# A decoder layer on one core: strided queries of the dilated attention copied, keys and values stored in runs of four tokens

## The chip, the cores and the metric

The kernel runs on one core of a Trainium2 chip. The metric is the device time of one launch in microseconds, the median of the runs shown. All arithmetic is in 32-bit floats (fp32, and fp32r for most products).

## The reference, cut to what matters

One inference step of one layer, for a prompt of 2048 tokens (width 1024) and for eight samples of four tokens. A normed input is projected to q, k, v and u; q, k, v feed an attention of 8 heads of 64, u a pooling mixer; then an output projection, a second norm and a convolutional feed-forward. The change touches the prompt's attention. It has three patterns per head, with dilation 1, 4 and 16: a query sees itself and up to 128 earlier tokens of the same residue. The core of it, cut:

```python
DIL_PATTERNS = ((128, 1), (512, 4), (2048, 16))

def _dilated_branch_prompt(q, k, v, dilation, slopes):
    qs = q.reshape(b, L, dilation, h, dh)          # L = s // dilation
    ...
    kb = jnp.concatenate([kp[:, :-1], kp[:, 1:]], axis=2)   # the block before, the block itself
    scores = jnp.einsum('bnqchd,bnkchd->bnchqk', qb, kb).astype(jnp.float32) * (HEAD_DIM ** -0.5)
    diff = qi + Q_BLOCK - ki
    valid = ((diff >= 0) & (diff <= N_STRIDED))[None] & (key_j >= 0)
    bias = -slopes[:, None, None] * (dilation * diff).astype(jnp.float32)[None]
    scores = jnp.where(valid[None, :, None, None], scores + bias[None, None, None], NEG)
    m = jnp.max(scores, axis=-1, keepdims=True)
    p = jnp.exp(scores - m)
    l = jnp.sum(p, axis=-1, keepdims=True)
    out = jnp.einsum('bnchqk,bnkchd->bnqchd', (p / l).astype(v.dtype), vb)
```

The three patterns are then merged with weights from their log-sums.

## The kernel before, in words

**Projection.** Sixteen tiles of 128 tokens are normed, turned and multiplied with W_in (`project`, three products per pair of 128 rows, high and low parts). `finish_qk` (L444) norms q and k per head; `spill_qk` (L466) turns a tile so that channels stand on the partitions, splits it into high and low part (ScalarE L472, VectorE L474) and stores both in DRAM (`qT_hi`, `qT_lo`, `kT_hi`, `kT_lo`, 512 x 2048). `finish_v` (L434) stores v row by row (`v_s`).

**Attention.** For a head, `load_head` (L227) brings queries and keys of all 2048 tokens into one tile `QK` (two such tiles): high and low parts of the queries one above the other, and the keys' high and low part, each twice. A pattern has sixteen blocks of 128 queries: pattern 0 sixteen consecutive blocks, pattern 1 four blocks of each of four residues, pattern 2 one block of each of sixteen residues. `views` (L238) cuts a block's operands out of the tile by a stride: one float in 4 (16 bytes) for pattern 1, one in 16 (64 bytes) for pattern 2. A block that has a predecessor reads 256 keys, one without 128; pattern 2 has no predecessors at all, pattern 1 in 12 of 16 blocks, pattern 0 in 15.

An item is two blocks of one head and pattern; 8 items make a pattern, 192 the stage. `advance(i)` (L310) issues three steps of three items:

- `scores` (L248) of item i: per block two products, queries as the stationary operand (loaded as weights), keys high and then low as the moving one (L262, L263); VectorE adds the bias table, whose columns are keys, and reduces a row to its minimum (L265); ScalarE takes the exponential (L267). Buffers: Sp 4, T 4, P 4.
- `turn` of item i-2: a transpose of each 128 x 128 of P (L275), copied out of PSUM by VectorE or, every fourth time, ScalarE (L278, L280).
- `values` of item i-3: the products with V (L296, two passes each); ScalarE copies the output (L300), GpSimd the row minima (L302, `st` to O); every fourth item of an odd head stores O (`store_o`).

Items go by head, pattern 0, 1, 2 (2, 1, 0 in the last head). The loop at L656 also issues the loads: the next head's queries and keys, V of the next pair of heads (`next_v`, `load_v` L176: pattern 0 one DMA, pattern 1 four, pattern 2 one, in rows of 512 bytes), rows of the feed-forward's parameters (tile `row`, three buffers) and parts of W_out (`rawo`, same buffers). SP issues nearly all DMAs, in order. GpSimd makes the bias table (L166), the ones beside V (L172, L173) and the copies of L302.

The rest (merge, output projection, feed-forward by chunks of 512 tokens, the sample group's attention in between) is not touched.

Of the kernel before, what the change touches and what calls it, by code (L numbers as in the profile page):

```python
# [9 lines left out]
F32 = mybir.dt.float32  # L10
# [7 lines left out]
P = 128  # L18
# [25 lines left out]
def kernel(ctx, tc, ins, cst, outs):  # L44
# [25 lines left out]
    # the sample group's columns of a product stand side by side, hi then lo: one pass takes both  # L70
# [23 lines left out]
    def norm_rows(pool, xt, g_bc, bufs, tag="xn"):  # L94
        """x * rsqrt(mean(x^2) + eps), times g_bc where given."""
        rows = xt.shape[0]
        xn = pool.tile([rows, DM], F32, tag=tag, name="xn", bufs=bufs)
        ss = pool.tile([rows, 1], F32, tag="ss", name="ss", bufs=2)
        nc.scalar.activation(xn, xt, AF.Square, accum_out=ss)
        r = rms_scale(pool, ss, 1, DM)  # L100
        if g_bc is None:
            nc.scalar.activation(xn, xt, AF.Copy, scale=r)
        else:
            nc.vector.scalar_tensor_tensor(out=xn, in0=xt, scalar=r, in1=g_bc[:rows], op0=ALU.mult, op1=ALU.mult)  # L104
        return xn
# [5 lines left out]
    def transpose_split(src, hi, lo):  # L111
        """src [n, DM] -> hi, lo [128, KT, n]."""
        n = src.shape[0]
        for h in range(2):
            tp = psum.tile([P, 4, P], F32, tag="tp", name="tp", bufs=4)
            for k in range(4):
                kk = 4 * h + k
                nc.tensor.transpose(tp[:, k, :n], src[:, kk * P:(kk + 1) * P], ident[:n, :n])  # L118
            split(hi[:, 4 * h:4 * h + 4, :], lo[:, 4 * h:4 * h + 4, :], tp[:, :, :n])
# [8 lines left out]
    class Later:  # L128
        """Work on the tensor engine that is issued some bursts of products after what it waits for."""
# [39 lines left out]
    def value_tile(pool, tag):  # L169
        """Pairs of heads, with a column of ones on either side (the sums of the weights)."""  # L170
        t = pool.tile([P, 16, P + 2], F32, tag=tag, name="V", bufs=3 if tag == "V" else 1)
        nc.gpsimd.memset(t[:, :, 0:1], 1.0)  # L172
        nc.gpsimd.memset(t[:, :, P + 1:P + 2], 1.0)  # L173
        return t

    def load_v(hp, p, t, blocks=slice(0, 16)):  # L176
        vs = v_s[:, hp * P:(hp + 1) * P]
        d = t[:, :, 1:P + 1]
        if p == 0:
            nc.sync.dma_start(d[:, blocks], vs.rearrange("(n i) f -> i n f", i=P)[:, blocks])  # L180
        elif p == 1:
            for J in range(4):
                nc.sync.dma_start(d[:, 4 * J:4 * J + 4, :], vs[J * CH:(J + 1) * CH].rearrange("(i c) f -> i c f", c=4))
        else:
            nc.sync.dma_start(d, vs.rearrange("(i c) f -> i c f", c=16))
# [4 lines left out]
    def param_load(j):  # L190
        n = 2 * NF if j < 4 else 2 * SB
        row = rows_of[j] = p2.tile([2 * NF, 4 * P], F32, tag="row", name="row", bufs=3)
        if j < 4:
            src = conv_b if j == 3 else conv_w[0, j:j + 1]
            nc.sync.dma_start(row[:, 0:P], src.rearrange("l (c p) -> (l c) p", p=P))
        else:
            nc.sync.dma_start(row[:n], stv[:, (j - 4) * 4 * P:(j - 3) * 4 * P])
# [28 lines left out]

    def load_head(h):  # L227
        qk, tab = qk_tile(), bias_table(h)
        load_qk(h, qk, slice(0, S))
        heads[h] = (*(qk[:, i, :] for i in range(3)), tab)  # L230

    pair_v, pair_o, heads = {}, {}, {}
# [4 lines left out]

    def views(h, p, idx):  # L238
        r = DILS[p]
        blk, c = divmod(idx, r)  # L240
        q, kh, kl = (x.rearrange("p (j c) -> p c j", c=r)[:, c, :] for x in heads[h][:3])
        lo = blk - 1 if blk else 0
        return (q[:, blk * P:(blk + 1) * P], kh[:, lo * P:(blk + 1) * P], kl[:, lo * P:(blk + 1) * P],
                ([idx - r] if blk else []) + [idx])
# [3 lines left out]
    def scores(it):  # L248
# [6 lines left out]
        Pt = pq.tile([P, 2, 2 * P], F32, tag="P", name="Pt", bufs=4)  # L255
        blocks = []
        for s in range(2):
# [6 lines left out]
            T = pq.tile([P, 2 * P], F32, tag="T", name="T", bufs=4)  # L264
# [44 lines left out]

    def advance(i):  # L310
        if i < len(items):
            attn[i] = scores(items[i])
        if 0 <= i - 2 < len(items):
            PTs[i - 2] = turn(items[i - 2], attn[i - 2])
        if 0 <= i - 3 < len(items):
            values(items[i - 3], attn.pop(i - 3), PTs.pop(i - 3))

# [1 line left out]
    right = ExitStack()  # L319
    pw = right.enter_context(tc.tile_pool(name="pw", bufs=1, side="right"))  # L320
    with tc.tile_pool(name="p1", bufs=1) as p1:
# [24 lines left out]
        def load_w(i):  # L346
            """Raw weights; the high part of the next ones takes their place."""
# [6 lines left out]
        def split_w(i):  # L354
            """hi + lo of gain * w."""
# [78 lines left out]
        def finish_v(t, j, ps):  # L434
# [3 lines left out]
            else:  # L438
                v = p1.tile([P, AW], F32, tag="t", name="v", bufs=4)
                nc.scalar.copy(v, ps)  # L440
                nc.sync.dma_start(v_s[t * P:(t + 1) * P, :], v)
# [24 lines left out]
        def spill_qk(t, j, a):  # L466
            tp = tp4(a)
            for i, dst in enumerate(((qT_hi, qT_lo), (kT_hi, kT_lo))[j]):
                s = p1.tile([P, 4, P], F32R, tag="qkh", name="qkh", bufs=3)
                if i == 0:  # L470
                    hi = s
                    nc.scalar.copy(hi, tp)  # L472
                else:
                    nc.vector.tensor_tensor(out=s, in0=tp, in1=f32(hi), op=ALU.subtract)  # L474
                nc.sync.dma_start(dst.rearrange("(a p) t -> p a t", p=P)[:, :, t * P:(t + 1) * P], f32(s))

        def window_sums(cur, g, pick, tag, shape, n):
            """Trailing sums over 2 << g columns by doubling; pick(tile, a, b) are the columns a..b-1."""
# [150 lines left out]
    # rows 0..15: the sample group's states (new ones take the place of the old), 16, 17: the prompt's  # L629
# [4 lines left out]
    def h_tile(k):  # L634
        """High and low part of 128 rows: of W_out at first, then of the normed tokens of a chunk."""
# [15 lines left out]
    with tc.tile_pool(name="p2", bufs=1, reuse_waits="tile") as p2:  # L651
# [3 lines left out]
        nc.vector.memset(stT[:, :, 2 * SB:], 0.0)  # L655
        for i in range(AHEAD, len(items) + 3):  # L656
            if i < len(items):
# [23 lines left out]
    with tc.tile_pool(name="p4", bufs=1, reuse_waits="tile") as p4:  # L681
# [163 lines left out]
        def cache_rows(c, b, n, p, near):  # L845
            """The 128 cached rows that query n of sequence b reads in pattern p, as [128, AW]."""
# [139 lines left out]
        def sample_mix():  # L986
            """Output projection, residual and norm of the sample group, then its columns hs_s."""
# [49 lines left out]
        def store_ffn_state(j):  # L1037
            """New states of 512 columns, the sample group's and the prompt's."""
# [18 lines left out]
        for c in range(NCHUNK):  # L1057
# [5 lines left out]
            def spread(pss, prompt, sample):  # L1063
                """Pairs (destination, PSUM source) of the prompt's and sample's columns."""
# [115 lines left out]
def _constants():  # L1180
# [4 lines left out]
    base = np.stack([np.where(ok, r * diff, BIG) for r in DILS]).astype(np.float32)  # L1185
    i = np.arange(P)
# [38 lines left out]
```

## Time and profile before

| | us |
|---|---|
| median of 3 runs | 2590.65 |
| lowest, highest | 2588.75, 2595.58 |
| profiled execution, span from first to last instruction | 2587.3 |
| projection, up to the first score product | 443 |
| attention of the prompt | 399 (443 to 842) |
| merge, output projection, feed-forward | 1745.3 |

Of the profiled execution the profile gives the span; its own time was not taken apart from the runs above. The engines are PE (TensorE products), PEld (its weight loads, which overlap products), DVE (VectorE), ACT (ScalarE), POOL (GpSimd) and SP (the queue that issues DMAs). TensorE is pipelined: the durations of its rows overlap, so the distance from one start to the next says what an instruction costs. A granted clock of 1.00 is 2.4 GHz, 0.50 is 1.2 GHz; a value between is a mean over a stretch.

### The profile page before, as it was taken

To read this page: it belongs to the slowest core of one execution; us is meant where nothing else is said; L and a number is where in the kernel's file an instruction comes from. 1 tells how busy PE (TensorE), PEld (TensorE's weight loads), DVE (VectorE), ACT (ScalarE), POOL (GpSimd) and SP (SyncE) were. 2 spreads that over 40 slices of the span, in tenths; PEclk is the share of its full clock that TensorE was granted. 3 is DMA by queue.
4 is the path that set the end of the run, shared out by engine and by line. 5 is a ranking of instruction groups with operands and counts; after the bars stand their busy time and mean duration, and the time that the engine had idled before them with its cause. 6 is when DMAs were issued, how large, how long until landed. Compare 5 with 4: busy or idle time off the path is not lost.

```text
span 2587.3 us, 35898 instructions
## 1 busy us (share of the span) xinstructions
PE 2556.2 (99%) x13310; PEld 2187.1 (85%) x13310; DVE 1727.8 (67%) x3819; ACT 1089.6 (42%) x2021; POOL 117.4 (5%) x160
## 2 busy tenths in 40 slices
PE   8999999999999999999999999999999999999999
PEld 5888887999999788788888888888888788999997
DVE  7444345555555676799887788887887666666665
ACT  6333232555555222434433464443444443444442
POOL 1111111000000200000000000000000000000000
PEclk9999999998998999999999999999999999999999
DMA  6333335765561897955557534447443337232321
GB/s 220 106 118 112 121 110 149 153 174 131 125 160 51 294 309 244 298 183 183 181 165 233 157 106 146 137 128 246 143 138 114 122 110 232 84 90 83 91 75 61
DMA packets 411738, 393.57 MB, mean 152 GB/s; under 512 B 15211, under 2 KB 318407, under 8 KB 408876
## 3 DMA queue, kind: packets, MB, share of 16 engines
q1 hardware_dynamic: 411340, 390.48, 49.8%
q8 instruction: 105, 1.72, 0.3%
q0 software_dynamic: 224, 0.80, 0.1%
q14 instruction: 69, 0.57, 0.1%
HBM read 305.70 MB, written 85.52 MB: 151 GB/s over the span
## 4 chain that ended last, share of the span: by engine, by line
PE 62%; DMA 1%; DVE 1%; issue 0%; ACT 0%; SPq 0%; POOL 0%; POOLq 0%
PE pu L973 38%; PE pd L1149 19%; PE po L752 3%; PE pd L1143 1%; DMA om<-o_s 0%; DMA h<-hn_s 0%; PE sacc L925 0%; PE sacc L924 0%; PE po L1006 0%; DMA raw<-in_w_up_dram 0%; PE tp L118 0%; DMA h_s<-ya 0%; PE tpf L1041 0%; DVE xn L104 0%; PE tpa L737 0%
## 5 line engine op out<-in xcount | busy, mean ns | idle before, releaser
L973 PE MATMUL pu<-h,w 128*128 128x512 f32 (+1 forms) x5232 | 989.0, 349 | 1.5 <-ACT w L108 1.0
L973 PEld LDWEIGHTS pu<-h,w 128*128 128x128 f32 x5232 | 849.9, 188 | 132.4 <-ACT w L108 1.4
L1149 PE MATMUL pd<-w,act 128*128 128x512 f32 x2112 | 490.2, 392 | 0.0
L1149 PEld LDWEIGHTS pd<-w,act 128*128 128x128 f32 x2112 | 396.6, 188 | 88.1
L108 ACT CAST w<-raw 128x1024 fp32r<-128x1024 f32 (+1 forms) x282 | 286.9, 1026 | 293.0 <-PE pd L1149 189.7
L109 DVE TENSOR_TENSOR w<-raw,w 128x1024 fp32r<-128x1024 f32 (+1 forms) x278 | 328.6, 1185 | 23.9 <-ACT w L108 23.7
L422 PE MATMUL ps<-W_hi,xh 128*128 128x512 f32 x1024 | 332.1, 397 | 1.3 <-ACT xh L108 1.3
L1117 DVE SCALAR_TENSOR_TENSOR cv<-ex,cw,cv 128x512 f32<-128x512 f32 x352 | 262.3, 745 | 29.7 <-ACT cv L1109 27.2
L1107 ACT COPY ex<-pu 128x512 f32<-128x512 f32 (+1 forms) x220 | 110.1, 501 | 350.7 <-PE pu L973 350.3
L265 DVE CUSTOM_DVE_ANT_0 T<-Sp,tab 128x256 f32<-128x256 f32 (+1 forms) x384 | 132.0, 365 | 186.1 <-PE Sp L263 142.2
L422 PEld LDWEIGHTS ps<-W_hi,xh 128*128 128x128 f32 x1024 | 192.2, 189 | 43.4 <-ACT xh L108 2.0
L267 ACT ACTIVATE Pt<-T,st 128x256 f32<-128x256 f32 (+1 forms) x384 | 164.9, 458 | 136.4 <-DVE st L265 134.9
L422 PE MATMUL ps<-W_lo,xh 128*128 128x512 f32 x512 | 202.6, 396 | 0.0
L1151 DVE TENSOR_TENSOR ya<-ya,pd 128x512 f32<-128x512 f32 x192 | 131.0, 683 | 103.7 <-PE pd L1149 102.9
L296 PE MATMUL Op<-V,PTs 128*128 128x65 f32 x1200 | 174.8, 281 | 0.7 <-DVE PTs L278 0.6
L262 PE MATMUL Sp<-QK 128*128 128x256 f32 (+1 forms) x384 | 170.0, 453 | 5.5 <-DMA QK<-kT_hi 3.1
L296 PEld LDWEIGHTS Op<-V,PTs 128*128 128x128 f32 x1200 | 170.0, 209 | 1.2 <-DVE PTs L278 0.7
L1109 ACT ACTIVATE cv<-pu,cw 128x512 f32<-128x512 f32 (+3 forms) x264 | 166.0, 649 | 0.0
L91 POOL TENSOR_TENSOR rs<-ms,mhalf 128x1 f32<-128x1 f32 (+3 forms) x68 | 76.4, 1124 | 1582.7 <-DVE stT L1110 1046.9
L263 PE MATMUL Sp<-QK 128*128 128x256 f32 (+1 forms) x384 | 145.4, 387 | 0.6 <-DMA QK<-kT_lo 0.6
L275 PE MATMUL tp<-ident,Pt 128*128 128x128 f32 x600 | 127.7, 299 | 0.0
L108 ACT CAST act<-cv 128x512 fp32r<-128x512 f32 x88 | 54.6, 621 | 159.4 <-DVE cv L1126 150.7
(220 smaller groups left out, 2637.6 us busy)
## 6 DMA issues: line engine op xcount, KB each, us to landing
raw<-in_w_up_dram SPq DMA_DIRECT2D x176, 512.0 KB
raw<-in_w_down_dram SPq DMA_DIRECT2D x80, 512.0 KB
hn_s<-w SPq DMA_DIRECT2D x16, 1024.0 KB
h<-hn_s SPq DMA_DIRECT2D x32, 512.0 KB
far<-in_cache_k_dram SPq DMA_DIRECT2D x64, 256.0 KB
far<-in_cache_v_dram SPq DMA_DIRECT2D x64, 256.0 KB
om<-o_s SPq DMA_DIRECT2D x16, 792.0 KB
raw<-in_w_in_dram SPq DMA_DIRECT2D x16, 512.0 KB
```

The source lines that it names most:

```text
L108: nc.scalar.copy(hi, src)
L109: (eng or nc.vector).tensor_tensor(out=lo, in0=src, in1=f32(hi), op=ALU.subtract)
L262: nc.tensor.matmul(Sp[:, s, :w], q, kh, start=True, stop=False)
L263: nc.tensor.matmul(Sp[:, s, :w], q, kl, start=False, stop=True)
L265: nc.vector.tensor_tensor_reduce(out=T[:, :w], in0=Sp[:, s, :w], in1=tab[:, p, 2 * P - w:], op0=ALU.add, op1=ALU.min, scale=1.0, scalar=3e ...
L267: nc.scalar.activation(Pt[:, s, :w], T[:, :w], AF.Exp, bias=st[:, i8:i8 + 1], scale=-1.0)
L296: nc.tensor.matmul(Op[:, i4, :], PT[:, j, :], pair_v[hp, p][:, b, v0:v0 + DH + 1], start=n == 0, stop=n == m - 1)
L422: nc.tensor.matmul(ps, xh[:, a, k, :], (W_hi, W_lo)[b][j, k // 2][:, k % 2, :], start=n == 0, stop=n == 3 * KT - 1)
L973: nc.tensor.matmul(ps[:, :n], w[:, a, k, :], hs[k][:, b, c0:c0 + n], start=i == 0, stop=i == 3 * KT - 1)
L1109: nc.scalar.activation(d, s, AF.Identity, bias=cw[:, 3, ct:ct + 1], scale=cw[:, 2, ct:ct + 1])
L1117: nc.vector.scalar_tensor_tensor(out=d, in0=e[j], scalar=cw[:, j, ct:ct + 1], in1=d, op0=ALU.mult, op1=ALU.add)
L1149: nc.tensor.matmul(ps, act[0][:, a, k, tau * P:(tau + 1) * P], wd[k][:, b, :], start=k == 0 and j == 0, stop=k == n - 1 and j == 2)
```

## The change

1. Queries of patterns 1 and 2 are copied by GpSimd, half a pattern (8 blocks, 128 x 1024 floats) at a time, into a tile `qs` (two buffers) in which the tokens of one residue stand in a row. The copy for a half is issued three items before its first item; the two for pattern 1 of head 0 before the loop.
2. Keys are stored in DRAM, and so loaded, in another order: within each 64 tokens, token 16 i + c stands at place 4 c + i. So four tokens of one residue modulo 16 stand in a row, and also four of one residue modulo 4. The order is made where `spill_qk` copies out of PSUM. `views` reads runs of four floats.
3. V is stored in the same order (two DMAs for a tile instead of one). Its loads for patterns 1 and 2 become four DMAs, of 32 partitions each, where there was one.
4. The bias table's columns of patterns 0 and 1 are put in the new order of the keys; pattern 2's order of keys is as before.
5. To make room, T, P and `row` have one buffer less each.

```diff
+RUN = 4
+RES = 16
...
-        elif p == 1:
-            for J in range(4):
-                nc.sync.dma_start(d[:, 4 * J:4 * J + 4, :], vs[J * CH:(J + 1) * CH].rearrange("(i c) f -> i c f", c=4))
         else:
-            nc.sync.dma_start(d, vs.rearrange("(i c) f -> i c f", c=16))
+            r, n = DILS[p], S // (P * DILS[p])
+            for J in range(n):
+                src = vs[J * P * r:(J + 1) * P * r].rearrange("(m c i) f -> i m c f", c=r, i=RUN)
+                for i in range(RUN):
+                    nc.sync.dma_start(d[i::RUN, r * J:r * (J + 1), :], src[i])
...
+    def spread_q(h, p, half):
+        qs = spread[h, p, half] = p2.tile([P, S // 2], F32R, tag="qs", name="qs", bufs=2)
+        q, r = heads[h][0], DILS[p]
+        if p == 1:
+            src = q[:, half * (S // 2):(half + 1) * (S // 2)].rearrange("p (b j c) -> p b c j", b=2, c=r)
+            dst = qs.rearrange("p (b c j) -> p b c j", b=2, c=r)
+        else:
+            src = q.rearrange("p (j c) -> p c j", c=r)[:, half * r // 2:(half + 1) * r // 2]
+            dst = qs.rearrange("p (c j) -> p c j", j=P)
+        nc.gpsimd.tensor_copy(dst, src)
...
+    def queries(h, p, idx):
+        if p == 0:
+            return heads[h][0][:, idx * P:(idx + 1) * P]
+        return spread[h, p, idx // 8][:, idx % 8 * P:(idx % 8 + 1) * P]
...
-        q, kh, kl = (x.rearrange("p (j c) -> p c j", c=r)[:, c, :] for x in heads[h][:3])
...
+        def keys(x):
+            if p == 0:
+                return x[:, lo * P:(blk + 1) * P]
+            return x.rearrange("p (m c i) -> p m c i", c=r, i=RUN)[:, lo * P // RUN:(blk + 1) * P // RUN, c, :]
...
-        Pt = pq.tile([P, 2, 2 * P], F32, tag="P", name="Pt", bufs=4)
+        Pt = pq.tile([P, 2, 2 * P], F32, tag="P", name="Pt", bufs=3)
...
-            T = pq.tile([P, 2 * P], F32, tag="T", name="T", bufs=4)
+            T = pq.tile([P, 2 * P], F32, tag="T", name="T", bufs=3)
...
+    SPREAD = 3
+
     def advance(i):
+        if i + SPREAD < len(items):
+            h, p, pr = items[i + SPREAD]
+            if p and pr % 4 == 0 and i + SPREAD >= 2 * AHEAD:
+                spread_q(h, p, pr // 4)
...
-                nc.sync.dma_start(v_s[t * P:(t + 1) * P, :], v)
+                n = RUN * RES
+                for g in range(2):
+                    nc.sync.dma_start(v_s[t * P + g * n:t * P + (g + 1) * n].rearrange("(c i) f -> i c f", i=RUN),
+                                      v[g * n:(g + 1) * n])
...
+                d, src = s, tp
+                if j == 1:
+                    d = s.rearrange("p a (g c i) -> p (a g) c i", c=RES, i=RUN)
+                    src = tp.rearrange("p a (g i c) -> p (a g) c i", c=RES, i=RUN)
                 if i == 0:
-                    hi = s
-                    nc.scalar.copy(hi, tp)
+                    hi = d
+                    nc.scalar.copy(hi, src)
                 else:
-                    nc.vector.tensor_tensor(out=s, in0=tp, in1=f32(hi), op=ALU.subtract)
+                    nc.vector.tensor_tensor(out=d, in0=src, in1=f32(hi), op=ALU.subtract)
...
+        for half in range(2):
+            spread_q(0, 1, half)
...
+    j = np.arange(P)
+    for p, tok in enumerate((j // 64 * 64 + j % RUN * RES + j % 64 // RUN, j // 16 * 16 + j % RUN * 4 + j % 16 // RUN)):
+        base[p] = base[p][:, np.concatenate([tok, P + tok])]
```

## Rows read from the trace of the kernel before

**Rows 1.** The page's first part: busy us (share of the span) xinstructions.

```profile
PE 2556.2 (99%) x13310; PEld 2187.1 (85%) x13310; DVE 1727.8 (67%) x3819; ACT 1089.6 (42%) x2021; POOL 117.4 (5%) x160
```

**Rows 2.** Busy table of two stages: stretch, length, engines, clock, DMA, GB/s.

```profile
0.00:443.00 443.00, 428.10 (x2054) 346.08 (x2054) 214.02 (x481) 165.14 (x309) 72.61 (x62) 1.00 0.41 130
443.00:842.00 399.00, 395.26 (x2593) 382.67 (x2593) 212.36 (x933) 213.69 (x533) 23.94 (x75) 0.89 0.57 137
```

**Rows 3.** Busy table: patterns 2, 0, 1, 2, 0; then head 7's 2.

```profile
480.00:494.60 14.60, 14.60 (x97) 14.39 (x96) 7.82 (x39) 8.37 (x24) 0.39 (x2) 1.00 0.01 3
494.60:509.40 14.80, 14.30 (x112) 12.88 (x113) 8.72 (x38) 8.59 (x21) 2.48 (x3) 1.00 0.94 200
509.40:527.20 17.80, 17.80 (x119) 17.40 (x117) 9.68 (x40) 9.50 (x24) 0.40 (x2) 1.00 0.63 161
527.20:543.50 16.30, 16.24 (x98) 15.69 (x98) 7.82 (x40) 8.29 (x23) 0.57 (x4) 0.86 0.45 124
543.50:558.90 15.40, 15.40 (x112) 15.18 (x112) 8.82 (x39) 8.68 (x21) 2.70 (x5) 0.82 0.87 199
...
792.50:809.60 17.10, 17.05 (x84) 16.12 (x83) 6.70 (x39) 7.84 (x25) 0.39 (x2) 0.50 0.01 2
```

**Rows 4.** Timeline, TensorE, pattern 0 of head 6: granted clock 0.50, later 1.00.

```profile
746.64 0.41 PE L262 MATMUL Sp<-QK 128*128 128x256 f32 x1
746.85 0.41 PE L263 MATMUL Sp<-QK 128*128 128x256 f32 x1
...
753.57 0.28 PE L262 MATMUL Sp<-QK 128*128 128x256 f32 x1
753.69 0.28 PE L263 MATMUL Sp<-QK 128*128 128x256 f32 x1
```

**Rows 5.** Timeline, TensorE, pattern 1 of head 2, granted clock 1.00.

```profile
569.64 0.42 PE L262 MATMUL Sp<-QK 128*128 128x256 f32 x1
569.88 0.42 PE L263 MATMUL Sp<-QK 128*128 128x256 f32 x1
```

**Rows 6.** Timeline, three engines, an item of pattern 2 of head 4, clock 1.00.

```profile
685.51 0.41 PE L262 MATMUL Sp<-QK 128*128 128x128 f32 x1
...
685.75 0.40 PE L263 MATMUL Sp<-QK 128*128 128x128 f32 x1
...
685.97 0.40 PE L275 MATMUL tp<-ident,Pt 128*128 128x128 f32 x2
...
686.17 0.89 ACT L267 ACTIVATE Pt<-T,st 128x128 f32<-128x128 f32 x2 [0.79 <-DVE st L265]
686.21 0.56 PE L296 MATMUL Op<-V,PTs 128*128 128x65 f32 x4
...
686.32 0.29 DVE L265 CUSTOM_DVE_ANT_0 T<-Sp,tab 128x128 f32<-128x128 f32 x1 [0.19 <-PE tp L275]
...
686.54 0.42 DVE L278 COPY PTs<-tp 128x256 f32<-128x256 f32 x1
...
686.68 0.47 PE L262 MATMUL Sp<-QK 128*128 128x128 f32 x1
```

**Rows 7.** Groups: weight loads, patterns 0, 1 (head 1), 2: busy, mean ns, idle.

```profile
L262 PEld LDWEIGHTS Sp<-QK 128*128 128x128 f32 x17 | 3.2, 198 | 1.4 <-DVE st L265 1.2
...
L262 PEld LDWEIGHTS Sp<-QK 128*128 128x128 f32 x17 | 5.2, 307 | 0.1
...
L262 PEld LDWEIGHTS Sp<-QK 128*128 128x128 f32 x17 | 5.0, 297 | 0.2
```

**Rows 8.** Waits of the attention: us in total, times, longest.

```profile
DVE T L265 <- PE Sp L263: 142.2, 170, 4.6
...
DVE T L265 <- ACT Pt L267: 3.3, 4, 1.0
```

**Rows 9.** Groups, GpSimd, 430 to 900 us: its one operation on 1024 columns.

```profile
L109 POOL TENSOR_TENSOR w<-raw,w 128x1024 fp32r<-128x1024 f32 x4 | 9.6, 2412 | 11.5 <-ACT w L108 11.5
```

**Rows 10.** Timeline, SP's queue: a load of V.

```profile
756.22 0.64 SPq L185 DMA_DIRECT2D V<-v_s  x1
```

More of the change, by code (lines that the diff above doesn't have):

```diff
@@ L191, in param_load @@
         n = 2 * NF if j < 4 else 2 * SB
-        row = rows_of[j] = p2.tile([2 * NF, 4 * P], F32, tag="row", name="row", bufs=3)
+        row = rows_of[j] = p2.tile([2 * NF, 4 * P], F32, tag="row", name="row", bufs=2)
         if j < 4:
@@ L230, in load_head @@
         heads[h] = (*(qk[:, i, :] for i in range(3)), tab)
-    pair_v, pair_o, heads = {}, {}, {}
+    pair_v, pair_o, heads, spread = {}, {}, {}, {}
     def next_v(hp, p):
@@ L240, in views @@
         blk, c = divmod(idx, r)
-        q, kh, kl = (x.rearrange("p (j c) -> p c j", c=r)[:, c, :] for x in heads[h][:3])
         lo = blk - 1 if blk else 0
-        return (q[:, blk * P:(blk + 1) * P], kh[:, lo * P:(blk + 1) * P], kl[:, lo * P:(blk + 1) * P],
-                ([idx - r] if blk else []) + [idx])
+        def keys(x):
+            if p == 0:
+                return x[:, lo * P:(blk + 1) * P]
+            return x.rearrange("p (m c i) -> p m c i", c=r, i=RUN)[:, lo * P // RUN:(blk + 1) * P // RUN, c, :]
+        return queries(h, p, idx), keys(heads[h][1]), keys(heads[h][2]), ([idx - r] if blk else []) + [idx]
     state = {}
@@ L671 @@
                     for k in ((8 * p + pr) // 3,):
-                        raw = p2.tile([P, CH], F32, tag="row", name="rawo", bufs=3)
+                        raw = p2.tile([P, CH], F32, tag="row", name="rawo", bufs=2)
                         nc.sync.dma_start(raw, wov[:, k, 0:CH])
```

## The prediction, made before the changed kernel ran

> **What bounds the kernel now.** I began with the page's busy line: over the whole span TensorE is busy 99%, VectorE 67%, ScalarE 42%, GpSimd 5% [rows 1]. A share over the span says little here, so next came the busy table by stage. The diff touches the prompt attention and the spills and stores that feed it; the rest, 842 us to the end, is issued as before. The attention runs from 443 to 842 us, 399 us, with TensorE busy 395, VectorE 212, ScalarE 214, GpSimd 24, a granted clock of 0.89 and DMA at 0.57 [rows 2]. TensorE is the bound, and no other engine is busy for much over half of the stage.
>
> Then I cut the attention by head and pattern [rows 3]. In every head pattern 0 (contiguous tokens) takes about 15 us, pattern 1 (every fourth) 18, pattern 2 (every sixteenth) 16. Pattern 2 has half the score columns, half the transposes and half the value products of pattern 0 and should take about half. So I looked at the starts of score products at full clock. In pattern 0 they follow each other every 0.12 us with 256 columns [rows 4]; in pattern 1 every 0.24 us, same instruction, same width, only the layout differs [rows 5]; in pattern 2 after 0.24 and 0.22 us with only 128 columns (685.51, 685.75, 685.97) [rows 6]. The weight load of the queries takes 198 ns in pattern 0, 307 in pattern 1 and 297 in pattern 2 [rows 7]: a load whose elements stand 16 bytes apart is slowed as much as one with 64, by 0.10 to 0.11 us, which is what a product of pattern 2 loses. That load paces the scores.
>
> **What the change does, part by part.**
>
> *Queries.* Patterns 1 and 2 read contiguous copies. The loads then cost what pattern 0 pays. That part is read directly from the rows.
>
> *Keys.* The moving side of patterns 1 and 2 becomes runs of four floats, 16 bytes, with jumps between. No row shows such a read. Below, the bound is the contiguous read, 0.12 us for 256 columns [rows 4]; above, it is today's spacing, 0.24 [rows 5], under which today's one-element read of 256 columns fits. For 128 columns today's read fits under 0.22 and half of 0.24 is 0.12, so in pattern 2 the keys would hardly matter. I take the lower end: the 16-byte and the 64-byte stride cost the loads the same [rows 7], so the jump's length is not what costs; how few elements come from one place is, and a contiguous row too moves on to a new 16 bytes after four floats. The Trainium skill, "Advanced Engine Details and Errata", section "SBUF Cachelines", says that SBUF is read in lines of 16 bytes, that repeated hits on one line run at full speed and that a new line for each access is penalised. By that rule the runs of four cost nothing, which is the sum below; without it the upper end holds, which is the first rival.
>
> The gain on TensorE: 32 score products per head and pattern, 8 heads, so 256 in each. Pattern 1: 256 x (0.24 - 0.12) = 30.7 us. Pattern 2: 256 x (0.23 - 0.12) = 28.2 us. Together **-58.9 us**.
>
> *What comes late next.* Pattern 0 shows what a stretch looks like when its scores are fast: TensorE's loads sit idle 1.4 us in one head's 14.8, 1.2 of it until VectorE has reduced a score [rows 7]; in pattern 1 it is 0.1. I charge pattern 1 the same 1.4 us. An item of pattern 2 (two blocks) becomes on TensorE 4 scores x 0.12, two transposes of 0.24 together (685.97 to 686.21) and four value products of 0.47 (to 686.68) = 1.19 us [rows 6]. ScalarE needs 0.89 us for two exponentials, and an output copy in every second item and a copy of the transposes in every fourth come on top; VectorE 2 x 0.29 + 3/4 x 0.42 = 0.90 with the reading of its accumulator on top [rows 6]. Three engines of nearly equal length in one chain don't run at 1.19. Below, the cost is nothing; above, it is today's item, 14.6 / 8 = 1.8 us [rows 3]. I take 1.35, for the rows of pattern 0 (a wait of a tenth) are nearest: 8 x 0.16 = 1.3 us more per head. Charge: 8 x (1.4 + 1.3) = **+21 us**. The same goes for buffers of T and P that shrink from four to three: VectorE waited 3.3 us in all for ScalarE to release T [rows 8], so this is inside the charge.
>
> *The clock.* Pattern 2's stretch has a clock of 1.00 in head 0 and lasts 14.6 us; in head 1 it has 0.86 and 16.3; in head 7 it has 0.50, the lower of the two levels (1.2 GHz), throughout, and 17.1. Pattern 0 behind it lasts 14.8 us at 1.00 and 15.4 at 0.82 [rows 3]. Stretches of pattern 1 between the two heads have 1.00. In the rows the lower level belongs to pattern 2 and to what follows it. With its scores at half their spacing pattern 2 becomes more like pattern 1, so I expect most dips to go: five heads like head 1, 1.3 each of the 16.3 - 14.6 = 1.7 (some of it is parameter transposes, which head 0 lacks), 17.1 - 14.6 = 2.5 in head 7, 15.4 - 14.8 = 0.6 in five stretches of pattern 0: **-12 us**. Bounds: 0, and a loss, which is a rival.
>
> *The copies.* 32 copies of 128 x 1024 on GpSimd. The nearest row is a two-input operation of that size, 2.4 us [rows 9]. Below 2.4; above, twice, 4.8, if the strided read doubles as the loads' does. A buffer comes free four items before its copy is needed: 7 us in pattern 1, 4 x 1.35 = 5.4 in pattern 2. Total 77 to 154 us on an engine with 24 us of work [rows 2]. Behind a copy in its queue stand the copies of the row minima, the ones of V and the bias table, all due items later. Cost nothing while a copy stays below 5 us; a copy of 6 would add about 1 us per head.
>
> *SP's queue.* V of patterns 1 and 2 needs 16 and 4 DMAs instead of 4 and 1, 60 more over four head pairs, each 0.64 us of SP [rows 10], 38 us. Bytes and the 512-byte pieces stay. For the first pair 15 x 0.64 = 9.6 us stand ahead of head 1's queries and keys; the DMAs are idle (0.01) from 480 us on and head 1 starts at 494.6 [rows 3], some 6 us earlier after the change, so about 8 us of cover: at most 1 or 2 us lost, once. V of a later pair is loaded some 20 items ahead.
>
> *The spills.* The keys' 16 copies and 16 subtractions out of PSUM read at a stride. A mean operation of the first stage takes 0.53 us on ScalarE (165 / 309) and 0.44 on VectorE [rows 2]; at three times that, 16 x 2 x 0.5 = 16 us more on either, in a stage of 443 us where they are busy 165 and 214: nothing. 16 more stores of V lie on SP there; nothing waits but the last, a microsecond at most.
>
> **Sum:** -58.9 + 21 - 12 = -50 us, and the profiled span of 2587.3 becomes 2537. The span lies 3.4 us below the median of the runs, 2590.65; the same outside it gives **2541 us**.
>
> **The rivals.**
> 1. *Runs of four are no better than single elements for the keys.* Then pattern 1's 24 wide products stay near 0.22 and only the eight narrow ones gain: 24 x 0.02 + 8 x 0.12 = 1.4 us per head instead of 3.8, so 19 us less gain, and TensorE, still the bound there, loses the 11 us of waits: 2549 us with the clock mended, 2561 without. For it: no row shows the read. Against: the stride's length doesn't matter in the loads.
> 2. *The chain through VectorE and ScalarE takes over.* Pattern 2 stays at 1.6 us an item and pattern 1 saves only 1.5 us: today's 16.3 [rows 3] becomes 12.8, so (1.5 + 3.5) x 8 = 40 us are saved in all: 2551 us, and about 2563 if the dips stay. For it: VectorE waits 142 us for scores [rows 8] and starts late on each. Against: 212 and 214 busy of 399 leave room.
> 3. *Slower: the clock.* TensorE, waiting for the other two, is granted the lower level not in dips but for much of the attention. There the contiguous scores stand 0.21 us apart instead of 0.12 [rows 4], no better than strided ones at full clock; if transposes and values slow down to the same 0.21, a head takes 96 x 0.21 for the scores, 75 x 0.21 for the transposes (31 + 28 + 16 blocks of keys) and 150 x 0.21 for the values (two passes) = 67 us, against about 50 today (399 / 8) and 44 after the change. The gain of 6 us per head is lost when 6 / 23, a quarter of the work, is done at that level; today 0.22 of the time is (a mean of 0.89 between 1.00 and 0.50), though in pattern 2 it costs less. At half of the work: 8 x (11.5 - 6) = +44, 2635 us. For it: the dips of today. Against: pattern 1 has 1.00 [rows 3].
> 4. *GpSimd late.* At 8 us a copy pattern 2 would wait 8 - 5.4 = 2.6 us per head: 21 us less gain, 2562.
> 5. *The order of the work moves.* The halved spacing might also shift when K, V and O transfers meet: the 0.57 of 399 us [rows 2] is 0.65 of 349; a few us.
>
> **Chances and range.** The forecast 0.60 (its own range 2518 to 2560: all waits gone and all of the clock regained is 2520, no clock gain 2553), rival 1 0.12, rival 2 0.14, rival 3 0.07, rival 4 0.04, rival 5 0.03. The range 2515 to 2570 takes in the first two rivals and most of the fourth. A measurement tells about 0.3%, 7.8 us, from no change. Only rival 3, and 1 or 2 together with 4, ends near or above 2583: faster 0.88, same 0.05, slower 0.07.
>
> **What would show it.** Score products of patterns 1 and 2 at 0.12 us spacing and query loads at 190 to 200 ns; pattern 1 at 15 us, pattern 2 at 12 to 13; the attention at about 350 us; copies of 2.4 to 5 us on GpSimd and no load on TensorE waiting for one. If pattern 1 stays at 0.21 with loads at 190, the keys failed. If scores are at 0.12 and TensorE waits for VectorE or ScalarE, the second rival holds. If the spacing is 0.21 and the clock 0.50, the third. I would be wrong altogether if the query loads stayed above 300 ns.

## The result, and the profile after

The changed kernel takes 2543.28 us (median; 2538.81 to 2545.03), beside 2589.73 us for the kernel before on the same chip: a ratio of 0.9815, 95% interval 0.9801 to 0.9829. The forecast was 2541 us. The total came out; three of its terms (the waits, the clock, SP's queue) did not, and that their errors cancelled was luck. All rows here are of a profiled execution of 2538.81 us, the shortest of the four runs, with a span of 2537.0.

The page's busy line, as in [rows 1], and the busy table of the three stages, as in [rows 2] (stretch, length, the five engines, granted clock, DMA share, GB/s):

```profile
PE 2497.4 (98%) x13310; PEld 2126.6 (84%) x13310; DVE 1729.4 (68%) x3819; ACT 1085.1 (43%) x2021; POOL 180.7 (7%) x192
```

```profile
0.00:444.80 444.80, 428.40 (x2054) 346.63 (x2055) 214.33 (x481) 164.75 (x309) 72.29 (x62) 1.00 0.41 129
444.80:790.00 345.20, 335.60 (x2596) 321.21 (x2597) 210.01 (x935) 209.75 (x534) 87.03 (x108) 0.91 0.65 159
790.00:2537.00 1747.00, 1733.41 (x8662) 1458.77 (x8661) 1305.01 (x2404) 710.61 (x1179) 21.34 (x23) 1.00 0.51 161
```

The attention fell from 399 us to 345.2, the first stage grew by 1.8, the rest by 1.7: 50.3 us in all. VectorE and ScalarE have the work that they had; GpSimd has 63 us more.

**Scores and loads.** The timeline of TensorE in pattern 1 of head 3 (256 columns) and in pattern 2 of head 2 (128 columns), both at a granted clock of 1.00, as in [rows 5] and [rows 6]; then the groups of weight loads of patterns 1 and 2 of head 3, as in [rows 7]:

```profile
595.71 0.28 PE L288 MATMUL Sp<-QK,qs 128*128 128x256 f32 x1
595.83 0.27 PE L289 MATMUL Sp<-QK,qs 128*128 128x256 f32 x1
...
565.10 0.28 PE L288 MATMUL Sp<-QK,qs 128*128 128x128 f32 x1
565.21 0.28 PE L289 MATMUL Sp<-QK,qs 128*128 128x128 f32 x1
```

```profile
L289 PEld LDWEIGHTS Sp<-QK,qs 128*128 128x128 f32 x31 | 5.9, 191 | 0.0
L288 PEld LDWEIGHTS Sp<-QK,qs 128*128 128x128 f32 x31 | 5.9, 190 | 0.4 <-DVE st L291 0.3
```

Products follow at 0.12 us (wide) and 0.11 (narrow) instead of 0.24 and 0.22; loads take 190 ns instead of some 300, and in both stretches together they wait 0.4 us.

**Heads.** The busy table of head 2 (patterns 0, 1, 2) and of head 3 (0, 1, 2), as in [rows 3]:

```profile
531.80:544.80 13.00, 13.00 (x113) 12.57 (x112) 8.67 (x40) 8.69 (x22) 4.71 (x6) 1.00 0.66 181
544.80:558.30 13.50, 13.49 (x117) 13.25 (x117) 9.50 (x40) 9.25 (x24) 2.31 (x3) 1.00 1.02 208
558.30:568.20 9.90, 8.71 (x68) 7.82 (x68) 5.88 (x32) 5.48 (x16) 4.32 (x4) 1.00 1.00 305
568.20:589.40 21.20, 21.20 (x150) 20.77 (x150) 10.52 (x45) 11.25 (x29) 4.50 (x4) 0.76 0.71 151
589.40:602.90 13.50, 13.50 (x121) 13.37 (x120) 9.74 (x42) 9.37 (x24) 2.47 (x5) 1.00 0.69 182
602.90:614.80 11.90, 11.85 (x102) 11.42 (x102) 7.72 (x40) 7.84 (x24) 4.47 (x6) 1.00 0.38 106
```

Pattern 1 takes 13.5 us, pattern 2 of an odd head 11.9: better than forecast. But pattern 2 of head 2 stands out: TensorE executes 68 instructions in it where head 3 has 102, and the next stretch has 150 and takes 21.2 us at a mean clock of 0.76. The timeline of TensorE shows what happens (in brackets: idle time and who ended it):

```profile
564.71 0.33 PE L288 MATMUL Sp<-QK,qs 128*128 128x128 f32 x1 [0.20 <-DVE st L291]
...
565.87 0.33 PE L288 MATMUL Sp<-QK,qs 128*128 128x128 f32 x1 [0.28 <-DVE st L291]
...
567.98 0.39 PE L288 MATMUL Sp<-QK 128*128 128x256 f32 x1 [0.50 <-DVE st L291]
568.20 0.32 PE L288 MATMUL Sp<-QK,qs 128*128 128x128 f32 x1
568.36 0.28 PE L289 MATMUL Sp<-QK,qs 128*128 128x128 f32 x1
568.47 0.44 PE L289 MATMUL Sp<-QK 128*128 128x128 f32 x2
568.75 0.55 PE L322 MATMUL Op<-V,PTs 128*128 128x65 f32 x4
```

From 564.2 to 568.5 us TensorE issues score products alone (those without qs, near the end, are the next head's) and waits for VectorE; transposes and values then come as a backlog, at a clock of 0.50 from 569.7 to 579.9. V was not late: SP's queue has its four transfers issued by 553.4 us (the 16 ahead of them take the 0.64 us each of [rows 10]), the semaphore steps of the last one end at 563.5, and the first product that uses them starts at 568.75. In the whole attention no wait of TensorE is put down to V; the value products have this one:

```profile
PE Op L322 <- DVE PTs L304: 0.6, 1, 0.6
```

SP's queue at V:

```profile
526.81 10.27 SPq L190 DMA_DIRECT2D V<-v_s  x16
...
544.70 8.74 SPq L190 DMA_DIRECT2D V<-v_s  x4
```

It is the order. In which order an engine takes its instructions is fixed when the kernel is built, and TensorE's list reads, at this place (a running number, line, operation, buffers, semaphores waited for; Sp_6960 belongs to an item of pattern 2 of head 2, QK_6469 is the next head's tile):

```
2717 L288 MATMUL Sp_6960<-QK_5851,qs_6843 128x128 [waits DVE_49]
2718 L289 MATMUL Sp_6960<-QK_5851,qs_6843 128x128
2719 L288 MATMUL Sp_7004<-QK_6469 128x128 [waits DMAHW5_49,DMAHW6_49,DMAHW4_49,DMAHW0_49]
2720 L288 MATMUL Sp_7024<-QK_6469 128x256
2721 L289 MATMUL Sp_7004<-QK_6469 128x128 [waits DMAHW7_49,DMAHW1_49]
2722 L289 MATMUL Sp_7024<-QK_6469 128x256
2723 L322 MATMUL Op_6910<-V_6502,PTs_6884 128x65 [waits DMAHW4_49,DMAHW3_49,DMAHW5_49,DMAHW2_49,Activation_49]
```

Counted over the lists, the first value products of pattern 2 stand 17 score blocks behind their own in heads 2, 4 and 6 (15 in head 0); in the kernel before, and in all odd heads of the changed one, about 7.

### The profile page after: what moved, and what is told of

Its sections match the earlier page's. It is cut to its first block, busy times and chain, and to the rows that moved or that the text cites. A ratio compares the mean times of both kernels' runs of the same rounds, so it can differ in the third digit from the quotient of the medians.

```text
span 2537.0 us, 36098 instructions
## 1 busy us (share of the span) xinstructions
PE 2497.4 (98%) x13310; PEld 2126.6 (84%) x13310; DVE 1729.4 (68%) x3819; ACT 1085.1 (43%) x2021; POOL 180.7 (7%) x192
## 4 chain that ended last, share of the span: by engine, by line
PE 94%; DMA 2%; DVE 2%; issue 1%; ACT 0%; POOL 0%; SPq 0%; DVEq 0%; ACTq 0%; POOLq 0%
PE pu L1014 39%; PE pd L1190 19%; PE ps L454 13%; PE po L793 6%; PE Op L322 5%; PE tp L301 3%; PE Sp L288 3%; PE Sp L289 2%; PE tp L122 1%; PE tp L463 1%; PE pd L1184 1%; DVE T L291 0%; PE pp L535 0%; DMA QK<-kT_lo 0%; DMA g_b<-in_g_q_dram 0%
## 5 line engine op out<-in xcount | busy, mean ns | idle before, releaser
L95 POOL TENSOR_TENSOR rs<-ms,mhalf 128x8 f32<-128x8 f32 (+3 forms) x68 | 76.4, 1124 | 1584.2 <-DVE stT L1151 1047.7
L454 PEld LDWEIGHTS ps<-W_lo,xh 128*128 128x128 f32 x512 | 96.9, 189 | 19.8
L1151 DVE COPY stT<-ex 128x2 f32<-128x2 f32 x176 | 28.9, 164 | 117.7 <-ACT ex L1148 117.5
```

What stands on the lines that cost most here:

```text
L454: nc.tensor.matmul(ps, xh[:, a, k, :], (W_hi, W_lo)[b][j, k // 2][:, k % 2, :], start=n == 0, stop=n == 3 * KT - 1)
```

## The experiments

The table holds all kernels. "Heads 0 to 5" runs from the first score product of the attention to that of head 6, "heads 6, 7" from there to the first one of the last item; the others are stretches of a pattern, in us.

| kernel | time | ratio to before, 95% interval | heads 0 to 5 | heads 6, 7 | head 2 p2 + head 3 p0 | head 5 p1 | head 5 p2 |
|---|---|---|---|---|---|---|---|
| before | 2589.73 | | 301.4 | 94.9 | 31.3 | 18.2 | 16.6 |
| changed | 2543.28 | 0.9815 (0.9801 to 0.9829) | 255.6 | 86.6 | 31.1 | 13.5 | 12.2 |
| 1, V of p2 from ScalarE | 2532.76 | 0.9788 (0.9772 to 0.9803) | 242.3 | 94.0 | 25.5 | 13.7 | 11.9 |
| 2, before with V cut | 2604.00 | 1.0063 (1.0048 to 1.0078) | 315.1 | 100.1 | 36.2 | 17.9 | 17.2 |
| 3, queries alone | 2546.16 | 0.9842 (0.9825 to 0.9858) | 260.1 | 89.3 | 31.2 | 16.1 | 12.3 |
| 4, keys alone | 2588.34 | 1.0003 (0.9991 to 1.0016) | 301.4 | 94.5 | 35.3 | 16.8 | 15.9 |
| 5, 1 + W_out in p1 | 2534.35 | 0.9793 (0.9778 to 0.9808) | 242.0 | 94.0 | 25.5 | 13.7 | 11.9 |
| 6, 1 + runs of two | 2551.93 | 0.9866 (0.9846 to 0.9886) | 262.1 | 90.9 | 26.0 | 16.2 | 12.8 |
| 7, 1 + copies twice | 2538.08 | 0.9812 (0.9794 to 0.9829) | 242.9 | 94.6 | 25.5 | 13.7 | 11.9 |
| 8, before, fewer buffers | 2585.57 | 0.9995 (0.9985 to 1.0004) | 302.6 | 90.3 | 33.8 | 18.1 | 16.5 |
| 9, 1 + W_out in head 7 | 2536.54 | 0.9800 (0.9785 to 0.9814) | 241.1 | 93.3 | 25.5 | 13.7 | 11.9 |
| 10, 1 + W_out held to head 7 | 2515.71 | 0.9717 (0.9704 to 0.9731) | 242.4 | 75.4 | 25.5 | 13.7 | 11.9 |

### 1. The order mended: V of pattern 2 from ScalarE's queue

```diff
                 for i in range(RUN):
-                    nc.sync.dma_start(d[i::RUN, r * J:r * (J + 1), :], src[i])
+                    (nc.scalar if p == 2 else nc.sync).dma_start(d[i::RUN, r * J:r * (J + 1), :], src[i])
```

> The changed kernel with one thing moved: the four transfers of V of pattern 2 are issued from ScalarE's queue instead of SP's. In the changed kernel's program the score products of pattern 2 in heads 0, 2, 4 and 6 stand up to 17 products ahead of the value products that belong to them (7 elsewhere), so that TensorE has only scores there and then a backlog; with this move they stand 7 ahead everywhere. Theory A (this order is what costs 5 to 8 us at the end of each even head): the stretches of pattern 2 of an even head and pattern 0 of the next, 30 to 33 us together, fall to about 25, and the time by some 26 us, to 2517. Theory B (the clock dips or the transfers cost it, whatever the order): 2538 to 2548.

Measured: 2532.76 us. The busy table of head 2's pattern 2 and head 3's pattern 0, then head 6's patterns 0, 1, 2 and head 7's first:

```profile
558.50:570.30 11.80, 11.75 (x102) 11.31 (x101) 7.61 (x40) 7.74 (x23) 4.31 (x4) 1.00 0.67 207
570.30:583.90 13.60, 13.47 (x116) 12.86 (x115) 8.80 (x40) 8.90 (x23) 4.56 (x4) 1.00 0.92 201
688.70:705.90 17.20, 14.54 (x110) 13.30 (x109) 9.44 (x41) 8.99 (x23) 4.61 (x6) 0.89 0.82 214
705.90:725.90 20.00, 20.00 (x124) 19.95 (x123) 9.49 (x39) 9.34 (x25) 2.31 (x3) 0.67 0.78 156
725.90:739.00 13.10, 11.98 (x100) 10.94 (x98) 11.19 (x45) 10.40 (x29) 4.70 (x4) 1.00 0.30 96
739.00:754.40 15.40, 14.49 (x82) 14.15 (x81) 7.57 (x40) 8.13 (x24) 4.79 (x4) 0.63 0.06 19
```

The total lies between the two theories, above the 2517 of A and below the range of B. In heads 1 to 5 theory A holds: 25.4 us instead of 31.1, 102 instructions where there were 68, and a clock of 1.00 from 456 to 702 us. Of the 13.3 us that heads 0 to 5 gain, heads 6 and 7 give 7.4 back. The waits of 688 to 740 us name what holds head 6, and the timeline of TensorE shows it:

```profile
ACT h L112 <- DMA rawo<-in_w_out_dram: 7.1, 4, 5.7
```

```profile
703.11 1.12 PE L301 MATMUL tp<-ident,Pt 128*128 128x128 f32 x4 [2.56 <-ACT Pt L293]
```

The cut of W_out into high and low parts stands in ScalarE's list among the exponentials, and its row's transfer is late: ScalarE stood still for 5.7 us, TensorE ran out of work for 2.6 of them, and was granted 0.50 from 702 to 719 us. The same shape as in the changed kernel, by another cause.

### 2. The order spoiled, in the kernel before

```diff
-                nc.sync.dma_start(d[:, 4 * J:4 * J + 4, :], vs[J * CH:(J + 1) * CH].rearrange("(i c) f -> i c f", c=4))
+                src = vs[J * CH:(J + 1) * CH].rearrange("(i c) f -> i c f", c=4)
+                for g in range(4):
+                    nc.sync.dma_start(d[g * 32:g * 32 + 32, 4 * J:4 * J + 4, :], src[g * 32:g * 32 + 32])
```

and the same for the one transfer of pattern 2.

> The kernel before, with nothing changed but the count of V's transfers: 16 for pattern 1 and 4 for pattern 2, of 32 partitions each, instead of 4 and 1. Layouts, bytes, queries and keys stay. Its program has the score products of pattern 2 in heads 0, 2, 4 and 6 up to 20 ahead of the value products. Theory A (the order costs): pattern 2 of each even head and pattern 0 of the next lose 4 to 8 us, 2605 to 2620. Theory B, the prediction's own step (60 more transfers on SP are hidden): 2588 to 2593.

Measured: 2604.00, 16 us slower, 1 us under theory A's range and 11 above theory B's. The busy table of head 2's pattern 2 and head 3's pattern 0:

```profile
582.50:595.00 12.50, 11.86 (x68) 11.12 (x68) 5.81 (x32) 6.00 (x17) 0.40 (x2) 0.89 0.00 0
595.00:618.70 23.70, 23.20 (x150) 22.38 (x150) 10.26 (x43) 10.37 (x26) 2.53 (x3) 0.70 0.63 134
```

The same 68 and 150 instructions as in the changed kernel, with nothing changed but the count of V's transfers. The DMAs are idle (0.00) all through the first stretch, so V had long landed: it is the order that costs, not the data. The prediction's step, that the 60 transfers cost at most 1 or 2 us, falls.

### 3. Queries alone

```diff
-            return x.rearrange("p (m c i) -> p m c i", c=r, i=RUN)[:, lo * P // RUN:(blk + 1) * P // RUN, c, :]
+            return x.rearrange("p (j c) -> p c j", c=r)[:, c, lo * P:(blk + 1) * P]
```

with the spills, V and the distance table as before.

> The changed kernel with the keys, V and the distance table laid out as before: only the queries are copied. The narrow products of pattern 2 should follow at 0.12 us. For the products of 256 columns of pattern 1, theory A (a key read at a stride of four costs as much as the matrix read of the queries did, so that runs of four are needed): about 0.22 us apart, a stretch of pattern 1 of 16 us, 2540 to 2555, the program's order being spoiled in head 2 alone. Theory B (the keys' stride costs nothing beside the load of the queries): 0.12 us, a stretch of 13.5 us, 2515 to 2530.

Measured: 2546.16; theory A. TensorE's timeline in pattern 1 of head 4:

```profile
638.52 0.41 PE L287 MATMUL Sp<-QK,qs 128*128 128x256 f32 x1
638.75 0.41 PE L288 MATMUL Sp<-QK,qs 128*128 128x256 f32 x1
```

0.23 us, though the queries are contiguous: single elements on the moving side cost as much as the strided load did, and pattern 1 takes 16.1 us, 2.4 more than in experiment 1. Pattern 2, with its 128 columns, gains all the same. The kernel also holds its own control: only head 2 has the long order, 31.2 us; head 4 has the short one, 26.1 (12.6 + 13.5).

### 4. Keys alone

```diff
-        return spread[h, p, idx // 8][:, idx % 8 * P:(idx % 8 + 1) * P]
+        blk, c = divmod(idx, DILS[p])
+        return heads[h][0].rearrange("p (j c) -> p c j", c=DILS[p])[:, c, blk * P:(blk + 1) * P]
```

and no copies.

> The changed kernel without the copies: keys, V and the distance table in runs of four, queries read at their stride from the tile of queries and keys. Theory A (the query load paces the scores): loads of some 300 ns, products 0.22 to 0.24 us apart as before, nothing gained, and the order of the even heads is as in the changed kernel, so 2590 plus some 20: 2600 to 2615. Theory B (the keys' layout is what pays): products of pattern 1 at 0.12 to 0.16 us, 2550 to 2575.

Measured: 2588.34, between the two ranges: under A's, above B's. The groups of weight loads from 620 to 740 us, and TensorE's timeline in pattern 1 of head 4:

```profile
L290 PEld LDWEIGHTS Sp<-QK 128*128 128x128 f32 x114 | 33.4, 297 | 0.0
L289 PEld LDWEIGHTS Sp<-QK 128*128 128x128 f32 x115 | 32.7, 287 | 2.5 <-DVE st L292 2.2
```

```profile
668.76 0.50 PE L289 MATMUL Sp<-QK 128*128 128x256 f32 x1
669.11 0.39 PE L290 MATMUL Sp<-QK 128*128 128x256 f32 x1
669.33 0.33 PE L323 MATMUL Op<-V,PTs 128*128 128x65 f32 x2
```

The loads are as slow as before, so theory A's mechanism holds; its size was off, since the stretches of pattern 1 became 1.3 us shorter (16.8 in head 5), which paid for the long order (35.3). In pattern 1 neither half brings half of the gain by itself: a wide product still costs 0.22 us or more while either side is read in single elements.

### 6. Runs of two

```diff
-RUN = 4
+RUN = 2
...
-                for g in range(2):
+                for g in range(4):
...
-(j // 64 * 64 + j % RUN * RES + j % 64 // RUN, j // 16 * 16 + j % RUN * 4 + j % 16 // RUN)
+(j // 32 * 32 + j % RUN * RES + j % 32 // RUN, j // 8 * 8 + j % RUN * 4 + j % 8 // RUN)
```

on top of experiment 1.

> The kernel of the first experiment with runs of two tokens instead of four: V's transfers of patterns 1 and 2 are half as many, keys stand in runs of 8 bytes. Runs of four are read at 0.12 us for 256 columns, single elements at 0.23. Theory A (each jump costs the same, and twice as many columns jump as could): about 0.17, a stretch of pattern 1 of 14.8 us instead of 13.6, 2541 to 2547. Theory B (8 bytes in a row are enough): 0.12 and 2528 to 2536. Theory C (only a whole 16 bytes pays): 0.23, a stretch of 16.2, 2551 to 2558.

Measured: 2551.93; theory C. TensorE's timeline in pattern 1 of head 3:

```profile
601.34 0.41 PE L288 MATMUL Sp<-QK,qs 128*128 128x256 f32 x1
601.57 0.42 PE L289 MATMUL Sp<-QK,qs 128*128 128x256 f32 x1
```

0.23 us for runs of 8 bytes, no better than single elements; 0.12 for runs of 16. The cost is not per jump.

### 7. Each copy twice

```diff
         nc.gpsimd.tensor_copy(dst, src)
+        nc.gpsimd.tensor_copy(dst, src)
```

> The kernel of the first experiment with each of the 32 copies on GpSimd made twice, one behind the other, some 4 us instead of 2. Theory A (the prediction's: hidden while a copy stays under 5 us): the time of the first experiment, 2529 to 2537. Theory B (TensorE waits for the copy's end): more than 2 us in each of the stretches of pattern 2, 2548 or more, and TensorE's loads wait for GpSimd in the trace.

Measured: 2538.08, 1 us above theory A's range and 10 below theory B's. The stretches are as in experiment 1 to 0.1 us from head 1 to head 5 (one is 0.3 shorter); head 0's pattern 1 is 1.4 us longer. The rest of the 5 us between the two medians is in no stretch of these heads, and the two profiled executions stand the other way round (2535.29 here, 2537.34 there). GpSimd's groups, and the only wait of TensorE for a copy from 456 to 700 us:

```profile
L243 POOL CAST qs<-QK 128x1024 fp32r<-128x1024 f32 x32 | 64.5, 2015 | 0.2
L242 POOL CAST qs<-QK 128x1024 fp32r<-128x1024 f32 x32 | 64.3, 2011 | 89.1 <-PE Sp L290 89.1
```

```profile
PE Sp L289 <- POOL qs L243: 1.2, 1, 1.2
```

The copies are hidden, with room for as much again.

### 8. Fewer buffers in the kernel before

```diff
-        Pt = pq.tile([P, 2, 2 * P], F32, tag="P", name="Pt", bufs=4)
+        Pt = pq.tile([P, 2, 2 * P], F32, tag="P", name="Pt", bufs=3)
```

and T, row and rawo likewise.

> The kernel before with nothing but the smaller counts of buffers of the change: T and P three instead of four, rows of W_out and of the parameters two instead of three. In its program the products of pattern 2 in head 2 stand up to 17 ahead of the values, as in the changed kernel; elsewhere the order is the old one. Theory A (order): 4 to 6 us in heads 2 and 3 and the rest as before, 2592 to 2596. Theory B, the prediction's step (buffers cost next to nothing): 2587 to 2590.

Measured: 2585.57; no change in total, so theory A's total falls, and theory B's range (2587 to 2590) is missed by 1.4 us. In the place of the long order, head 2 into head 3, it lost 33.8 - 31.3 = 2.5 us, again with idle DMAs; heads 6 and 7 were 4.6 us shorter, for a reason that no run settles.

```profile
577.10:589.80 12.70, 12.27 (x69) 11.52 (x70) 5.85 (x32) 5.32 (x15) 0.40 (x2) 0.87 0.00 0
```

### 5, 9 and 10. W_out out of ScalarE's way

What is left in experiment 1 is head 6. All three stand on top of experiment 1. The fifth kernel cuts W_out in patterns 1 of heads 6 and 7; the ninth, with the same kind of edit, in head 7 alone:

```diff
-                if h == 6 and (8 * p + pr) % 3 == 0:
...
+                if h >= 6 and p == 1 and pr % 2 == 0:
+                    k = 4 * (h - 6) + pr // 2
+                    rawo[k] = p2.tile([P, CH], F32, tag="row", name="rawo", bufs=2)
+                    nc.sync.dma_start(rawo[k], wov[:, k, 0:CH])
```

> The kernel of the first experiment (V of pattern 2 issued from ScalarE) with one thing more: the eight rows of W_out, cut in eight steps over head 6, are cut in the stretches of pattern 1 of heads 6 and 7, where TensorE has most to do, and each is loaded three steps ahead of its cut. In the first experiment heads 1 to 5 take 39 us each, head 6 takes 50 with ScalarE held 5.7 us by the load of one row, and the first two patterns of head 7 run at a clock of 0.50. Theory A (ScalarE held by W_out's loads, and its work in pattern 2, are what head 6 and 7 lose): head 6 at 39 to 40, the time 12 to 16 us below the first experiment, 2517 to 2521. Theory B (the end of the attention loses this to the transfers whatever ScalarE does): 2529 to 2535.

> The kernel of the first experiment with the eight rows of W_out loaded and cut in head 7 alone, one every second item from the end of its pattern 2 on, each loaded four items ahead. In the fifth experiment they were issued in head 6 behind the last head's queries, keys and V, whose transfers kept the DMAs full until 719 us, and the first row's cut held ScalarE for 5.3 us there. In head 7 no other transfer of the pairs is left. Theory A (ScalarE held by a late row of W_out is what heads 6 and 7 lose): heads 6 at 39 to 40, pattern 2 of head 7 at 12 to 13, no granted clock of 0.50 between 460 and 760 us, and 2515 to 2523. Theory B (the last heads lose it to something else): the lower clock and the long stretches stay, 2529 to 2535.

Measured: 2534.35 and 2536.54, no gain (the ninth lies 1.5 us above theory B's range). By the times alone theory B would stand. But the waits of the fifth and of the ninth, from 680 us on, show that the edit had not done what it was to do:

```profile
ACT h L112 <- DMA rawo<-in_w_out_dram: 5.6, 2, 5.3
```

```profile
ACT h L112 <- DMA rawo<-in_w_out_dram: 4.2, 1, 4.2
```

In the fifth, four of the eight cuts were written into head 6, and in ScalarE's list seven stand there; in the ninth all were written into head 7, and the build had moved six up into head 6. In both the first one stands at the end of head 6's pattern 1, where the row lands only once the transfers of the last queries, keys and V are through (719 us). The tenth kernel makes that impossible: the rows take the buffers of the copies of head 7, which come free only there.

```diff
+                if n in (12, 16, 17, 20):
+                    j = (12, 16, 17, 20).index(n)
+                    rawo[j] = p2.tile([P, 2, CH], F32, tag="qs", name="rawo", bufs=2)
+                    nc.sync.dma_start(rawo[j], wov[:, 2 * j:2 * j + 2, 0:CH])
```

where n counts the items of head 7.

> The kernel of the first experiment with W_out's rows loaded into the buffers that the copies of the queries leave in head 7. So no cut can stand earlier on ScalarE than the middle of that head's pattern 1; in the fifth and the ninth experiment the first cuts still stood in head 6 in ScalarE's order and held it for 5.3 and 4.2 us until the row had landed. Theory A (a late row of W_out holds ScalarE, TensorE runs out of work, and what follows is done at the lower clock): head 6 at 39 to 40, pattern 2 of head 7 at 12 to 13 and pattern 1 at 14, no granted clock of 0.50 from 460 to 760 us, 2517 to 2525. Theory B (the last heads lose it to something else): long stretches in heads 6 and 7 with a clock of 0.50, 2530 to 2537.

Measured: 2515.71, ratio 0.9717: theory A, 1.3 us under its range, and a version that beats both kernels. The first cut now stands in head 7's pattern 1, and the granted clock is 1.00 from 470.4 to 784.4 us; a dip of 3.4 us at 467 is left. The busy table of the attention, then head 6's three patterns and head 7's first two (2 and 1):

```profile
446.00:769.00 323.00, 315.47 (x2617) 301.93 (x2617) 210.48 (x935) 208.98 (x535) 87.29 (x108) 0.98 0.70 171
```

```profile
689.30:702.90 13.60, 13.07 (x110) 12.12 (x108) 8.87 (x39) 8.12 (x22) 4.59 (x6) 1.00 0.80 199
702.90:716.90 14.00, 13.96 (x124) 13.72 (x123) 9.35 (x39) 9.64 (x25) 2.32 (x3) 1.00 1.07 218
716.90:728.30 11.40, 11.35 (x99) 11.02 (x98) 7.47 (x39) 7.77 (x23) 4.18 (x4) 1.00 0.11 22
728.30:737.80 9.50, 9.50 (x83) 9.36 (x82) 6.31 (x39) 7.12 (x23) 4.35 (x4) 1.00 0.01 2
737.80:749.50 11.70, 11.70 (x103) 11.40 (x101) 8.03 (x38) 8.65 (x23) 2.42 (x3) 1.00 0.54 162
```

Heads 6 and 7 take 75.4 us instead of 94.0. Some of that is W_out's cuts leaving patterns 2 and 1: head 7's, at 9.5 and 11.7 us, are shorter than theory A had them (12 to 13, 14), and than head 5's, which turn parameters.

## Why the prediction was right, and where it was not

- **Queries and loads: right.** 190 ns and 0.12 us, as forecast. Experiment 4 shows that nothing much comes without them.
- **Keys: right, and one of the two reasons given fits.** The lower end of the bound holds: runs of four read like contiguous ones, which too move on to a new 16 bytes after four floats. The other reason, that few elements from one place are what costs, would have put runs of two between; they cost as much as single elements (experiment 6). Experiment 3 prices the first rival: 2.4 us per head, which is the 3.8 - 1.4 that the rival gave. The Trainium skill, "Advanced Engine Details and Errata", section "SBUF Cachelines", says that repeated hits on one line of 16 bytes run at full speed and that a new line for each access is penalised; the 0.12 us of runs of four and the 0.23 of single elements agree. It also asks for at least two hits on a line to hide the memory's delay, by which runs of two would do; experiment 6 has two hits on each line, and the products stay 0.23 us apart. The measurement decides: here runs of four were needed.
- **The waits, +21 us: wrong.** Pattern 1 fell by 18.2 - 13.5 = 4.7 us in head 5, where 3.8 of scores less 1.4 of waits were forecast (what gave the 0.9 beyond the scores is open); pattern 2 of head 0, at full clock in either kernel, from 14.6 to 11.0 in experiment 1, 3.6 us, which is the 28.2 / 8 = 3.5 of the scores and nothing against it. The step that failed: the 0.16 us per item was charged on top of a stretch whose 1.8 us per item already held the same slack. Its parts, 4 x 0.23 + 0.24 + 0.47, give 1.63 [rows 6]. The item forecast at 1.35 measures 11.0 / 8 = 1.37; the sum should have gone from 1.8 to 1.35, not from 1.8 less the scores plus 0.16.
- **SP's queue: wrong, and the term that cancelled it.** "V of a later pair is loaded some 20 items ahead" was a count of time on the chip, and even that was generous (the program issues it 12 items ahead). It was in time on the chip. What the 20 transfers moved was the order written into TensorE's list. In the kernel before it costs 16 us by itself (experiment 2); taken out of the changed kernel, heads 0 to 5 are 255.6 - 242.3 = 13.3 us shorter (experiment 1). That the build works with an estimate of when each transfer lands, and found V late, is the reading that fits the three things that changed the order (the count of transfers, the queue they are issued from, the counts of buffers); the estimate itself was not seen.
- **The clock: right in kind, not in full.** The dips behind the odd heads are gone; those behind the even heads stayed, and in each TensorE had just been idle in a run of scores. The time at 0.50 within the attention fell from 85 us to 65; in experiment 1 it is 48, in experiment 10 it is 10, at a mean of 0.98 instead of 0.89. What makes the clock fall stays open: in the kernel before it fell in pattern 2 of head 1 (0.86) although TensorE was idle for 0.06 us of 16.3 there [rows 3].
- **The rivals.** None of the four larger ones came. The fifth, "the order of the work moves", was the one that did, at a chance of 0.03 and "a few us", and through the order of the list, where it had been thought of as transfers that meet.
- **Copies: right that they are hidden** (experiment 7); at 2.0 us each they lie under the lower bound of 2.4. The upper bound, twice that "as the loads' does", misread the loads, which take 1.5 times as long when strided (307 to 198 ns). **Buffers: right in total** (experiment 8).
- **Spills: too low.** Attention begins at 444.8 to 446.9 us in the eight kernels that spill in the new layout, and at 441.7 to 444.7 in the four that do not (before, 2, 3, 8): about 3 us by the means (446.0 and 442.9), where a microsecond at most was forecast. Which of the copies or stores costs it was not tried.

In heads 0 to 5, where no cut of W_out stands, the layout with its order mended is worth 301.4 - 242.3 = 59 us (experiment 1). By the sum 58.9 x 6/8 = 44 of them are scores; the rest was not taken apart, but the time at 0.50 fell from 55 to 10 us there. The whole attention is 399 - 323 = 76 us shorter in experiment 10; how much of that the kernel before would gain from W_out's cuts in the same place was not tried.

## What to carry to other kernels

A change to transfers can cost through the order of another engine's instructions, with every transfer in time: compare how far each stage stands ahead of the next in the lists of both kernels, and in the trace look for stretches with too few instructions followed by ones with too many. When a stretch is rebuilt from parts, check first that the parts of today's stretch add up to today's length, and charge only for slack that is not in it already. Where an edit to an order brings nothing, look whether the build kept the order; a buffer that comes free late holds it, a place in the source does not.

## What was not expected of the hardware

- The moving side of a score product of 256 columns: 0.23 us in single floats and in runs of two, 0.12 in runs of four; no step between.
- With 128 columns, single floats 64 bytes apart cost nothing beside the load: 0.11 us in pattern 2 of experiment 3, as in the changed kernel.

```profile
650.40 0.29 PE L288 MATMUL Sp<-QK,qs 128*128 128x128 f32 x1
650.51 1.04 PE L321 MATMUL Op<-V,PTs 128*128 128x65 f32 x8
```

- A copy of 128 x 1024 floats on GpSimd takes 2.0 us whether its elements stand 16 or 64 bytes apart (1.95 to 2.34 over 32 of them).
- A short gap was followed by a long dip: in the changed kernel TensorE was idle 1.15 us from 563.5 to 568.5 us, and then ran at 0.50 for 10 us.
